# How many weight halves are split ahead in the second block of a fused two-block transformer

## The chip, the cores and the metric

The kernel runs on one core of one Trainium2 chip. The metric is device time in microseconds (us); smaller is better. Three runs of the kernel before took 713.87, 714.85 and 716.04 us, a median of 714.85 us.

## The reference

One sequence of 256 tokens, 1024 wide, in float32, goes through two blocks. Block 1 is an RMS norm, a stick-breaking attention beside a gated short convolution, and a mixture of 32 experts. Block 2 is the one that the change touches:

```
h = x @ w_in_2                          # 1024 -> 2560, split into q, k, v, u, z of 512 each
qh, kh = rope(q), rope(k)
attn = causal softmax(qh kh^T / 8) v    # 8 heads of 64
u, z = gelu(u), gelu(z)
sg = u * (tril(w_s) layer_norm(z) + b)  # per group of 64, in chunks of 128 tokens
merged = [rms_norm(attn), rms_norm(sg)]
x = layer_norm(alpha * x + merged @ w_out_2)
ffn = (silu(x @ w_gate) * (x @ w_up)) @ w_down      # hidden width 2816 = 22 chunks of 128
x = layer_norm(alpha * x + ffn)
```

## The kernel before

**Weights.** Every weight reaches the chip as a tile of 128 x 2048 float32, 1 MB. `Feed` (line 53) holds the tiles' order and a ring of buffers. Whenever a buffer is given back (`done`), the next tile's transfer is put on the SP queue. In block 2 the ring has six buffers.

**Splits.** Block 2 multiplies in float32r, with each operand as a high and a low part. `Split` (line 91) makes the parts of a weight half (128 x 1024) with two instructions of `hi_lo` (line 257): ScalarE copies the half into `whi` (L258), and VectorE subtracts that copy from the half into `wlo` (L259). The parts lie in nine buffers in block 2 (`WBUF2`), so half k+9 can be written only when TensorE has done with half k. `get(name)` hands out the next half. Before that it calls `ahead(n_got + n - less)`, which writes into the program the splits of all halves up to n ahead of the one handed out, with n = 9: the whole pool. `proj_tok` (L292) takes four halves for a projection of 512 columns, 12 matmuls of 512 columns each (L271). Behind the matmuls of half u it calls `ahead` once more and then the steps that the caller gave for that place (`then[u]`).

**Order of block 2.** The projections come as z, q, k, u, v (L1099 to L1115), 20 halves, numbered 0 to 19 here. Into them are woven, as `then` steps, the work on finished projections. Of these the prediction uses the path of z: `z_mean`, `z_sq` and `z_rstd` find each group's mean and deviation (the power of -1/2 runs on GpSimd, `rsqrt`, L249); `z_scale` (L981) multiplies on VectorE (L984), then multiplies and adds the layer norm's gain and bias on GpSimd (L985, L986); `z_mix(0)` (L988), the step behind the third half of k, multiplies the result by the spatial weights on TensorE (L992). `rope` (L941) turns q and k on VectorE, and adds on GpSimd (L951). Then follow the output projection (`wo2`, halves 20 to 27), the first layer norm (L1173 to L1247), and the feed-forward part, whose halves begin at 28. The first four of these are used inside the layer norm's section (`first_hidden`, L1212). At its end, L1247 splits up to nine ahead of half 32, so halves 33 to 40, since 32 is there by then. Then `gated(0)` and `gated(1)` (L1253) reduce the four results of `first_hidden`, which frees their PSUM banks, and `hidden(2)`, `hidden(3)` (L1264) do the next two hidden chunks. `hidden(3)` uses the two `pc` banks that `gated(1)` frees.

**Who sets the order.** Inside `tc.manual_schedule(...)` the named engines keep their instructions in the order of the program: around the whole z projection (L1089 to L1099) and around the layer norm (L1173 to L1247). Elsewhere a planner orders each engine's instructions: it plays the program through with times of its own, and gives an engine that has come free the instruction that stands earliest in the program among those that it takes to be ready. Each engine then runs its instructions strictly in the order so found.

Of the kernel before, what the change touches and what calls it, by code (L numbers as in the profile page):

```python
# [33 lines left out]
WBUF = 3  # L34
WBUF2 = 9
# [17 lines left out]
class Feed:  # L53


    def __init__(self, nc, order):
        self.nc = nc
        self.order = order
        self.free = []
        self.loaded = []  # L60
        self.n_loaded = 0
        self.slot = {}
# [18 lines left out]
    def get(self, name):  # L81
        _, t, s = self.loaded.pop([n for n, _, _ in self.loaded].index(name))
        self.slot[id(t)] = s
        return t
# [6 lines left out]
class Split:  # L91


    def __init__(self, feed, pool, units, hi_lo, n):
        self.feed, self.pool, self.units, self.hi_lo, self.n = feed, pool, units, hi_lo, n
        self.held = {}
        self.ready = []
        self.n_got = 0
# [11 lines left out]
            self.ready.append((name, hi, lo))  # L110

    def get(self, name, less=0):
        self.ahead(self.n_got + self.n - less)
        got, hi, lo = self.ready[self.n_got]
        assert got == name, (got, name)
        self.n_got += 1
        return hi, lo
# [3 lines left out]
def fused_blocks(ctx: ExitStack, tc: tile.TileContext, a, out):  # L121
# [10 lines left out]
    def pool(name, bufs=1, side=None, **kw):  # L132
        es = ExitStack()
        p = es.enter_context(tc.tile_pool(name=name, bufs=bufs, side=side, reuse_waits="tile", **kw))
        return es, p


    units_a, units_b, order = [], [], []
# [74 lines left out]
    feed = Feed(nc, order)  # L213
# [29 lines left out]
    def small(p, w, tag, bufs=2):  # L243
        ctr[0] += 1
        return p.tile([P, w], F32, tag=tag, name=f"{tag}_{ctr[0]}", bufs=bufs)
# [19 lines left out]
    def dense_tok(acc, ks, cols, xh, xl, t, first, last):  # L265

        tok = slice(t * P, (t + 1) * P)
        for i, (kc, hi, lo, o) in enumerate(ks):
            for n, (x_, w_) in enumerate(((xh, hi), (xh, lo), (xl, hi))):
                for c in cols:  # L270
                    mm(acc[c], x_[:, kc, tok], w_[:, o + c * 512:o + (c + 1) * 512],  # L271
                       start=first and i == 0 and n == 0, stop=last and i == len(ks) - 1 and n == 2)
# [18 lines left out]

    def proj_tok(W, name, xh, xl, then={}, new=bank):  # L292
        accs = [[new()] for _ in range(NT)]
        for u in range(4):
            hi, lo = W.get(name)
            for t in range(NT):
                dense_tok(accs[t], [(2 * u, hi, lo, 0), (2 * u + 1, hi, lo, 512)], (0,), xh, xl, t, u == 0, u == 3)
            if u in then:
                W.ahead(W.n_got + W.n)
                then[u]()  # L300
        return [c[0] for c in accs]

    def rows_proj(W, name, acc, xh, xl, k0, first, last, then={}):

        if not last:
            for u in range(2):
                hi, lo = W.get(name)
                for t in range(NT):
                    dense_tok(acc[t], [(k0 + u, hi, lo, 0)], (0, 1), xh, xl, t, first and u == 0, False)
                if u in then:  # L310
                    W.ahead(W.n_got + W.n)
                    then[u]()
            return
        ks = [(k0 + u,) + W.get(name, 2 * u) + (0,) for u in range(2)]
        for t in range(NT):
            for c in range(2):
                dense_tok(acc[t], ks, (c,), xh, xl, t, first, True)
                if 2 * t + c in then:
                    then[2 * t + c]()
# [34 lines left out]
    wes, wp = pool("w_a", bufs=WBUF, side="left")  # L354
# [20 lines left out]
    W = Split(feed, wp, units_a, two_halves, WBUF)  # L375
# [541 lines left out]
    wes, wp = pool("w_b", bufs=WBUF2, side="left")  # L917
    xes, xp = pool("x_b", side="left")
    ees, ep = pool("blk2", side="right")
    W = Split(feed, wp, units_b, hi_lo, WBUF2)  # L920
    x_hl = xp.tile([P, 2, KD, S], F32R, name="x2")
    xh, xl = x_hl[:, 0], x_hl[:, 1]
    mh = xp.tile([P, KD, S], F32R, name="mh2")
# [38 lines left out]
    def gelu(n, dst):  # L962
        for t in range(NT):
            act(dst[:, t, :], b2[n][t], AF.Gelu)
# [120 lines left out]
    def then(*steps):  # L1085

        return {i: (lambda fs=fs: [f(*a) for f, *a in fs]) for i, fs in enumerate(steps)}

    with tc.manual_schedule(engines=in_order):  # L1089
# [7 lines left out]
        for k in range(0, KD, 2):  # L1097
# [12 lines left out]
    v_sb = ep.tile([P, NT, 512], F32, tag="x2T1", name="v2")  # L1110
    gelu("u2", u_sb)
    nc.scalar.preload_act_table_set("natural_log_exp_and_others")
    b2["v2"] = proj_tok(W, "v2", xh, xl, then([(z_gate, 0), (soft_b, 0)], [(soft_a, 1), (z_gate, 1), (soft_c, 0)],
                                              [(soft_b, 1), (z_t, 0)], [(soft_d, 0), (soft_a, 2), (soft_c, 1)]))
    v_in()  # L1115
# [16 lines left out]
    def attn_rows(t, us, cols):  # L1132
        for u in us:
            dense_tok(acc[t], ks[u:u + 1], cols, mh, ml, t, u == 0, u == 3)
# [12 lines left out]
    def stats(t, c, combine):  # L1147
        if c == 0:
            ln[t] = fp.tile([P, 2, 6], F32, tag="bst", name="bst", bufs=2)
        o = xres[:, t, c * 512:(c + 1) * 512]  # L1150
        combine(t, c, o)
        nc.vector.bn_stats(out=ln[t][:, c, :], in_=o)  # L1152
        if c:
            mv = small(fp, 2, "mv")
            nc.vector.bn_aggr(out=mv, in_=ln[t])
            ve = small(fp, 1, "ve")
            ts(ve, mv[:, 1:2], 1e-5, None, op0=ALU.add)
            ln[t] = mv[:, 0:1], rsqrt(fp, ve)
# [14 lines left out]
    with tc.manual_schedule(engines=in_order):  # L1173
        for c in range(2):
            attn_rows(0, (3,), (c,))
            stats(0, c, add_mix)
        shift = small(fp, 1, "mr")
        stt(out=shift, in0=ln[0][0], scalar=-1.0, in1=ln[0][1], op0=ALU.mult, op1=ALU.mult)
        attn_rows(1, (0, 1), (0, 1))
        for cols in half:  # L1180
            act(xn[:, 0, cols], xres[:, 0, cols], AF.Identity, scale=ln[0][1], bias=shift)
        attn_rows(1, (2, 3), (0,))
        stats(1, 0, add_mix)

        def turned(src, t, k, z):

            for i in range(2):
                tr(z[:, k % 4 + i, :], src[:, t, (k + i) * P:(k + i + 1) * P], ident)

        def in_chunks(z):  # L1190
            return z.rearrange("p (k s) -> p k s", k=4)

        z0 = [in_chunks(bank_c()) for _ in range(2)]
        for j in range(4):
            turned(xn, 0, 2 * j, z0[j // 2])
        attn_rows(1, (2, 3), (1,))
        ws = [[W.get("fgu", 4 + 2 * f + i) for i in range(2)] for f in range(2)]
        zs = [[two_parts(new()) for _ in range(2)] for new in (bank, bank_c)]

        def split3(t, j, src):  # L1200
            ks = slice(2 * j, 2 * j + 2)
            hi_lo(xh[:, ks, tok[t]], xl[:, ks, tok[t]], src)

        def part0(j):

            x3 = fp.tile([P, 2, P], F32, tag="x3", name="x3", bufs=2)
            for i in range(2):
                kc = 2 * j + i
                act(x3[:, i, :], z0[j // 2][:, kc % 4, :], AF.Identity, scale=V("ln1_g", kc), bias=V("ln1_b", kc))
            split3(0, j, x3)  # L1210

        def first_hidden(t, j):  # L1212

            for kc in (2 * j, 2 * j + 1):
                f = slice(kc * P, (kc + 1) * P)
                for w, z in zip(ws, zs):
                    for (hi, lo), z_ in zip(w, z):
                        mm(z_[:, :, tok[t]], hi[:, f], both(x_hl, kc, tok[t]), start=kc == 0 and t == 0, stop=False,  # L1218
                           skip_group_check=True)
                        if t:  # L1220
                            mm(z_[:, 0, :], lo[:, f], xh[:, kc, :], start=False, stop=kc == KD - 1,
                               skip_group_check=True)

        ln1 = feed.get("ln1")
        g1, b1 = ln1[:, 0:D], ln1[:, D:2 * D]
        part0(0)
        stats(1, 1, lambda t, c, o: (add_mix(t, c, o), part0(1)))
        part0(2)
        centred(1, half[0], g1)
        part0(3)  # L1230
        for j in range(4):
            first_hidden(0, j)
        z1 = [in_chunks(bank_c()) for _ in range(2)]

        def part1(j):
            scaled(xres[:, 1, quarter[j]], 1, quarter[j], b1)
            turned(xres, 1, 2 * j, z1[j // 2])

        part1(0)
        for j in range(4):  # L1240
            if j < 3:
                part1(j + 1)
            split3(1, j, z1[j // 2][:, 2 * (j % 2):2 * (j % 2) + 2, :])
            if j == 0:
                centred(1, half[1], g1)
            first_hidden(1, j)
        W.ahead(W.n_got + W.n)  # L1247


    acc = None  # L1250
# [146 lines left out]
```

## Time and profile before

| what | value |
|---|---|
| median of three runs | 714.85 us (713.87 to 716.04) |
| the profiled execution | 713.62 us |
| its span, from the first to the last instruction | 711.9 us |
| TensorE busy | 661.3 us, 93% |
| VectorE busy | 368.2 us, 52% |
| ScalarE busy | 271.1 us, 38% |
| mean granted TensorE clock | 0.978 |

Times in the rows are microseconds from the start of the span. PE is TensorE's matmuls, DVE is VectorE, ACT is ScalarE, POOL is GpSimd. A row of a timeline shows the start, the duration, the engine, the line, the operation with what it writes and reads, and in brackets how long the engine had been idle before it and what ended the wait. "x16" means that 16 instructions are merged into the row. Matmuls are pipelined, so a row's duration can reach into the next. Block 2 begins with the matmul at 403.53 us and takes the rest of the span.

### The profile page before, as it was taken

The page shows a single profiled execution, that of the slowest core. Times are in us where ns is not written, and L with a number is a line of the kernel's source. Part 1 is how long each engine was busy: PE and PEld are TensorE (multiplying, and loading weights), DVE is VectorE, ACT ScalarE, POOL GpSimd, SP SyncE. Part 2 cuts the span into 40 slices and gives each one's busy share as a digit, 9 for nine tenths or more (in the row PEclk, how much of TensorE's full clock was granted, in tenths as well). Part 3 has the DMA queues.
Part 4 walks back from the last instruction along what each step waited for, and adds up shares of the span by engine and source line. Part 5 has one row for each costly group of instructions (what it writes and reads, how often), then busy time and mean ns, then how long its engine had stood idle before and what let it go on. Part 6 is the DMA issues. An engine that isn't in the chain of part 4 may idle for free. (4 is left out here: it accounts for less than half of the span.)

```text
span 711.9 us, 10413 instructions
## 1 busy us (share of the span) xinstructions
PE 661.3 (93%) x4249; PEld 516.7 (73%) x4249; DVE 368.2 (52%) x578; ACT 271.1 (38%) x413; POOL 43.9 (6%) x60
## 2 busy tenths in 40 slices
PE   8999999999999888998799598999979999999995
PEld 6888999999964444434256386877778888888884
DVE  6657555555521211212000488577578767667646
ACT  6567554444310000000000583477364444444410
POOL 2321100000000000000000006001100000000001
PEclk9999999999999999999899799999999999999998
DMA  8983479738879999999999784542146655555001
GB/s 341 410 338 119 147 303 347 258 122 344 365 298 394 421 420 419 419 420 417 418 418 416 269 319 155 193 162 66 54 180 234 231 189 192 200 193 178 1 0 60
DMA packets 27558, 185.63 MB, mean 261 GB/s; under 512 B 3312, under 2 KB 3824, under 8 KB 5872
## 3 DMA queue, kind: packets, MB, share of 16 engines
q1 hardware_dynamic: 27504, 184.89, 67.2%
q8 instruction: 36, 0.59, 0.3%
q14 instruction: 18, 0.15, 0.1%
HBM read 183.83 MB, written 1.05 MB: 260 GB/s over the span
## 5 line engine op out<-in xcount | busy, mean ns | idle before, releaser
L259 DVE TENSOR_TENSOR wlo<-w,whi 128x1024 fp32r<-128x1024 f32 (+1 forms) x151 | 185.4, 1237 | 84.3 <-ACT whi L258 83.1
L258 ACT ACTIVATE whi<-w 128x1024 fp32r<-128x1024 f32 (+1 forms) x151 | 157.3, 1057 | 165.9 <-PE pa_t L271 67.9
L286 PE MATMUL pc_t<-x,whi 128*128 128x512 f32 x320 | 114.9, 402 | 3.8 <-DVE fs L1255 3.8
L287 PE MATMUL pc_t<-x,wlo 128*128 128x256 f32 x320 | 90.4, 282 | 0.0
L286 PEld LDWEIGHTS pc_t<-x,whi 128*128 128x128 f32 x320 | 60.8, 190 | 19.0 <-ACT fs L1256 4.1
L806 PE MATMUL pc_t<-w,xg 128*32 128x512 f32 x512 | 62.0, 617 | 4.0 <-DMA w<-in_w_gu_dram 4.0
L287 PEld LDWEIGHTS pc_t<-x,wlo 128*128 128x128 f32 x320 | 61.1, 191 | 0.4
L836 ACT ACTIVATE h<-pc_t 128x256 f32<-128x256 f32 x8 | 3.1, 384 | 135.2 <-PE pc_t L755 110.5
L756 DVE TENSOR_TENSOR xg<-pc_t,vec 128x512 f32<-128x512 f32 (+2 forms) x18 | 11.4, 633 | 80.2 <-PE pc_t L755 80.2
L806 PEld LDWEIGHTS pc_t<-w,xg 128*32 128x32 f32 x512 | 14.5, 111 | 39.6 <-issue 26.0
L271 PE MATMUL pa_t<-whi,x 128*128 128x512 f32 x128 | 42.8, 403 | 0.0
L847 PEld LDWEIGHTS pa_t<-st,y 128*128 128x128 f32 x128 | 23.0, 189 | 21.9 <-DVE y L863 12.5
L847 PE MATMUL pa_t<-st,y 128*128 128x256 f32 x128 | 31.9, 392 | 6.3 <-DVE y L863 6.2
L280 PE MATMUL pc_t<-xh,wlo 128*128 128x256 f32 x128 | 36.2, 283 | 0.0
L279 PE MATMUL pc_t<-xl,whi 128*128 128x256 f32 x128 | 36.2, 283 | 0.0
L278 PE MATMUL pc_t<-xh,whi 128*128 128x256 f32 x128 | 36.2, 283 | 0.0
L806 PE MATMUL pc_t<-w,hT 128*32 128x512 f32 (+1 forms) x272 | 31.2, 574 | 4.1 <-ACT hT L842 4.1
L755 PEld LDWEIGHTS pc_t<-pr,xres 128*128 128x128 f32 x256 | 29.3, 192 | 7.8 <-PE pc_t L806 4.2
L755 PE MATMUL pc_t<-pr,xres 128*128 128x128 f32 x256 | 31.1, 278 | 0.9 <-DVE pr L746 0.9
L863 DVE COPY y<-pc_t 128x512 f32<-128x512 f32 x7 | 4.8, 692 | 50.8 <-PE pc_t L806 50.8
L271 PE MATMUL pa_t<-whi,fh 128*128 128x512 f32 x88 | 28.7, 392 | 0.0
L271 PE MATMUL pa_t<-wlo,fh 128*128 128x512 f32 x88 | 28.6, 391 | 0.0
(313 smaller groups left out, 1225.6 us busy)
## 6 DMA issues: line engine op xcount, KB each, us to landing
w<-in_w_gu_dram SPq DMA_DIRECT2D x64, 1024.0 KB, 19.4
w<-in_w_dn_dram SPq DMA_DIRECT2D x32, 1024.0 KB, 19.6
w<-in_w_in_dram SPq DMA_DIRECT2D x28, 1024.0 KB, 12.6
w<-in_w_ffn_dram SPq DMA_DIRECT2D x22, 1024.0 KB, 4.9
w<-in_w_fdn_dram SPq DMA_DIRECT2D x11, 1024.0 KB, 4.8
w<-in_w_out_dram SPq DMA_DIRECT2D x8, 1024.0 KB, 5.0
w<-in_w_in_dram SPq DMA_DIRECT2D x4, 512.0 KB, 12.2
w<-in_w_cv_dram SPq DMA_DIRECT2D x2, 1024.0 KB, 9.4
```

The lines of the kernel that those rows point to most:

```text
L258: act(hi, src, AF.Copy)
L259: tt(out=lo, in0=src, in1=hi.bitcast(F32), op=ALU.subtract)
L271: mm(acc[c], x_[:, kc, tok], w_[:, o + c * 512:o + (c + 1) * 512], start=first and i == 0 and n == 0, stop=last and i == len(ks) - 1 and n ...
L278: mm(acc, hi[:, f], xh[:, kc, :], start=kc == 0, stop=False)
L279: mm(acc, hi[:, f], xl[:, kc, :], start=False, stop=False)
L280: mm(acc, lo[:, f], xh[:, kc, :], start=False, stop=kc == nk - 1)
L286: mm(z, hi[:, f], x[:, :, kc, :], start=kc == 0, stop=False, skip_group_check=True)
L287: mm(z[:, 0, :], lo[:, f], x[:, 0, kc, :], start=False, stop=kc == nk - 1, skip_group_check=True)
L755: mm(zv[:, k, :], xres[:, t, kc * P:(kc + 1) * P], pr[:, t, :], start=t == 0, stop=t == 1)
L756: tt(out=xg[:, ks, :], in0=zv, in1=V("ffn_g")[:, ks].unsqueeze(2).to_broadcast([P, n, P]), op=ALU.mult)
L806: mm(out[sl, 0:n], x[:, sl], w[:, e * 512 + i * n:e * 512 + (i + 1) * n], start=start, stop=stop, skip_group_check=True)
L847: mm(acc[2 * c + k // 2][:, k % 2, :], ys[c][:, k * P:(k + 1) * P], st, start=False, stop=False, skip_group_check=True)
```

## The change

`Split` gets a distance `lead` of its own and a step `grow`. In block 2 `lead` begins at 5 (`WBUF + 2`) in place of 9, while the pool keeps its nine buffers. Ahead of the v projection `grow` is set to 1, so that each further `get` raises `lead` by one until it is 9. Each `get` in v then writes two splits into the program. At the end of the layer norm, L1247 no longer splits eight halves: it sets `lead` to 2, and from there every `get` raises it by one again. Block 1's `Split` has no `lead` given and works as before.

```diff
-    def __init__(self, feed, pool, units, hi_lo, n):
+    def __init__(self, feed, pool, units, hi_lo, n, lead=None):
         self.feed, self.pool, self.units, self.hi_lo, self.n = feed, pool, units, hi_lo, n
+        self.lead = lead or n
+        self.grow = 0
...
     def get(self, name, less=0):
-        self.ahead(self.n_got + self.n - less)
+        self.lead = min(self.n, self.lead + self.grow)
+        self.ahead(max(self.n_got + 1, self.n_got + self.lead - less))
...
             if u in then:
-                W.ahead(W.n_got + W.n)
+                W.ahead(W.n_got + W.lead)
                 then[u]()
...
-    W = Split(feed, wp, units_b, hi_lo, WBUF2)
+    W = Split(feed, wp, units_b, hi_lo, WBUF2, WBUF + 2)
...
     nc.scalar.preload_act_table_set("natural_log_exp_and_others")
+    W.grow = 1
     b2["v2"] = proj_tok(W, "v2", xh, xl, then([(z_gate, 0), (soft_b, 0)], [(soft_a, 1), (z_gate, 1), (soft_c, 0)],
...
             first_hidden(1, j)
-        W.ahead(W.n_got + W.n)
+        W.lead = 2
```

## Rows read from the trace of the kernel before

**Rows 1.** The page's first part, TensorE to GpSimd: busy us, share of the span, instructions.
```profile
PE 661.3 (93%) x4249; PEld 516.7 (73%) x4249; DVE 368.2 (52%) x578; ACT 271.1 (38%) x413; POOL 43.9 (6%) x60
```
**Rows 2.** TensorE's waits from 400 to 712: us in total, times, longest.
```profile
PE pc_t L286 <- DVE fs L1255: 3.8, 1, 3.8
PE pc_t L992 <- POOL z L986: 3.2, 1, 3.2
```
**Rows 3.** Windows: length, busy us of PE, PEld, DVE, ACT, POOL; granted clock; DMA.
```profile
440.00:450.00 10.00, 9.16 (x45) 8.03 (x46) 5.42 (x7) 2.03 (x3) 3.33 (x3) 0.83 0.32 104
...
530.00:540.00 10.00, 6.23 (x28) 5.17 (x28) 10.00 (x16) 6.28 (x10) 0.00 (x0) 0.83 0.88 327
```
**Rows 4.** The chain that ended last, around the first gap: start, us, what.
```profile
421.27 10.91 PE pa_t L271 x48
...
436.93 1.66 POOL z L985
438.66 2.13 POOL z L986
440.84 2.64 PE pc_t L992 x16
443.49 3.78 PE pa_t L271 x12
...
453.60 1.73 PE pc_t L992 x16
```
**Rows 5.** GpSimd's timeline from 390 to 445.
```profile
393.80 1.10 POOL L959 TENSOR_SCALAR_AFFINE_SELECT w<-w 128x1024 f32<-128x1024 f32 x1 [205.28 <-DMA w<-in_w_sp_dram]
429.31 4.01 POOL L249 TENSOR_TENSOR rs<-ms,mhalf 128x8 f32<-128x8 f32 x2 [34.41 <-DMA w<-in_w_out_dram]
...
442.83 1.27 POOL L986 TENSOR_TENSOR z<-z,w 128x512 f32<-128x512 f32 x1
```
**Rows 6.** VectorE's timeline from 430 to 440.
```profile
430.59 1.23 DVE L259 TENSOR_TENSOR wlo<-w,whi 128x1024 fp32r<-128x1024 f32 x1
...
433.31 2.35 DVE L259 TENSOR_TENSOR wlo<-w,whi 128x1024 fp32r<-128x1024 f32 x1 [0.23 <-ACT whi L258]
...
436.18 0.68 DVE L984 TENSOR_TENSOR z<-z,rs 128x512 f32<-128x512 f32 x1
...
437.38 2.29 DVE L259 TENSOR_TENSOR wlo<-w,whi 128x1024 fp32r<-128x1024 f32 x1
```
**Rows 7.** ScalarE's timeline, a split in the k projection.
```profile
437.65 1.06 ACT L258 ACTIVATE whi<-w 128x1024 fp32r<-128x1024 f32 x1 [1.66 <-PE pa_t L271]
```
**Rows 8.** TensorE's timeline from 520 to 538.
```profile
520.92 0.48 PE L286 MATMUL pc_t<-x,whi 128*128 128x512 f32 x1
...
529.93 0.40 PE L286 MATMUL pc_t<-x,whi 128*128 128x512 f32 x1
...
530.28 0.40 PE L286 MATMUL pc_t<-x,whi 128*128 128x512 f32 x1
...
534.56 0.77 PE L286 MATMUL pc_t<-x,whi 128*128 128x512 f32 x1 [3.77 <-DVE fs L1255]
...
537.64 0.28 PE L287 MATMUL pc_t<-x,wlo 128*128 128x256 f32 x1
```
**Rows 9.** ScalarE's timeline behind the layer norm.
```profile
522.36 9.58 ACT L258 ACTIVATE whi<-w 128x1024 fp32r<-128x1024 f32 x10
```
**Rows 10.** VectorE's timeline, layer norm and behind it.
```profile
507.42 0.75 DVE L1161 SCALAR_TENSOR_TENSOR xres<-pa_t,rs,xres 128x512 f32<-128x512 f32 x1 [0.57 <-PE pa_t L271]
...
521.62 0.42 DVE L259 TENSOR_TENSOR x<-pc_t,x 128x256 fp32r<-128x256 f32 x1 [3.13 <-ACT x L258]
...
523.44 9.18 DVE L259 TENSOR_TENSOR wlo<-w,whi 128x1024 fp32r<-128x1024 f32 x8 [0.52 <-ACT whi L258]
532.53 0.68 DVE L1255 TENSOR_REDUCE fs<-pa_t 128x256 f32<-128x512 f32 x1
```
**Rows 11.** The window of the v projection, columns as in Rows 3.
```profile
462.00:478.00 16.00, 16.00 (x91) 12.16 (x87) 11.74 (x29) 13.07 (x32) 1.24 (x2) 1.00 0.46 164
```

More of the change, by code (lines that the diff above doesn't have):

```diff
@@ L310, in rows_proj @@
                 if u in then:
-                    W.ahead(W.n_got + W.n)
+                    W.ahead(W.n_got + W.lead)
                     then[u]()
@@ L1246, in fused_blocks @@
             first_hidden(1, j)
-        W.ahead(W.n_got + W.n)
+        W.lead = 2
     acc = None
```

## The prediction

> **What bounds the kernel now.** The page's first part comes first: TensorE is busy 93% of the span and VectorE 52% [rows 1], so a change on VectorE and ScalarE pays only where TensorE waits for them. Next I read TensorE's waits in block 2. Two of them touch code that the change moves: 3.8 us on VectorE's reduce of the first gated chunks (L1255), and 3.2 us on GpSimd's last step on z (L986) [rows 2]. The chain of waits and the timelines then show what stands in front of each.
>
> At the first gap `z_mix(0)` starts at 440.84, as soon as L986 is over [rows 4]. L986 and L985 follow `z_scale(0)`, which VectorE runs only at 436.18, behind two `wlo` splits, at 430.59 and 433.31. A third split runs beside GpSimd's two steps [rows 6]. GpSimd had both powers done at 433.32 (429.31 + 4.01) [rows 5], the first, which is the one needed, by about half of that pair, 431.3.
>
> At the second gap VectorE runs eight `wlo` in a row from 523.44, and the first reduce of `gated(0)` only behind them, at 532.53 [rows 10]; ScalarE runs ten `whi` [rows 9]. TensorE needs the banks of `gated(1)` for its next chunk and stands still for 3.77 us [rows 8].
>
> Behind each gap TensorE is also granted less clock: 0.83 in the mean of each of the two windows [rows 3], so a part of each stretch is at 1.2 and the rest at 2.4 GHz.
>
> **The change part by part.** No split is removed: in both kernels 1.06 us of ScalarE [rows 7] and about 1.23 us of VectorE [rows 6] per half. What changes is where each split stands in the program. The planner need not leave it there. It moves work far forward when it takes its input to be there: GpSimd's mask of the spatial weights (L959, written behind the z projection) runs at 393.80, ahead of block 2 [rows 5], and matmuls of `hidden(2)` run at 520.92, inside the layer norm [rows 8]. All nine buffers stay, so a split can still float forward to where its buffer comes free. What it loses is its rank: a split that stands later no longer beats a step that is ready at the same time.
>
> *The v-projection end of it, and the transfers.* Four splits fewer stand in z, and four more in v (two with each `get`). At the place in v this is 4 x 1.06 = 4.2 us of ScalarE and 4 x 1.23 = 4.9 us of VectorE. In the 16 us of v these have 2.93 and 4.26 us free [rows 11]. If all four stayed there, ScalarE would be over by 1.3 and VectorE by 0.7 us; 1.3 us is the upper end. I take 0, since the window before has VectorE idle for 4.58 of 10 us and ScalarE for 7.97 [rows 3], and the splits can float into it; the halves ready in stock (five at least) are a second cover. A tile's transfer follows its second half's split, so transfers start up to two tiles later; the DMA share is 0.46 in v and 0.32 before it [rows 11, 3], so I take 0 there too. The lower end is 0 for both: no wait of TensorE in v is there to be removed.
>
> *The first gap.* A half of a projection takes 12 matmuls of 10.91 / 48 = 0.227 us, 2.73 us [rows 4], and with each half one split falls due in either kernel, so VectorE's load between 429 and 438 need not fall. But in program order the splits written by then now stand behind `z_scale(0)`: with `lead` 9 those at 430.59 and 433.31 were ahead of it. Without these two, `z_scale(0)` comes 1.23 + 2.35 = 3.58 us earlier, at 432.6, and the power was ready at 431.3. That covers the gap of 3.23 us. Further, ScalarE's in-order queue stands behind a `whi` that waits 1.66 us for TensorE to give a buffer back [rows 7]; the squares of z were queued behind such waits, and they come earlier too. The least is a gain of 0, if the splits keep their places by floating. The most is the whole gap: 3.23 us, and the slow clock behind it. For that, `z_mix` took 2.64 instead of 1.73 us (0.91), and the next 12 matmuls 3.78 instead of 2.73 (1.05) [rows 4]. Together 3.23 + 1.96 = 5.2 us. I take all of it, since the work removed from the front is longer than the gap. What is late next is the second half of z: its last step ends at 442.83 + 1.27 = 444.1 [rows 5] and its `z_mix` runs at 453.60 [rows 4], so it has over 9 us to spare, some 4 of them after TensorE has moved forward by 5.2.
>
> GpSimd's add took 2.13 us beside the third split [rows 4] and 1.27 us with VectorE out of the way [rows 5]; a `wlo` took 2.35 beside GpSimd and 1.23 without [rows 6]. The Trainium skill (page "SBUF — State Buffer", section "Who interferes with whom") says of this that a VectorE instruction with two SBUF inputs and a GpSimd instruction that reads SBUF share a port, and whichever starts first holds it while the other blocks; the two rows agree. The rule speaks against the change, as it leaves a floated `wlo` free to land ahead of either step of GpSimd: by it each would wait up to 1.23 us, so L985 and L986 would take up to 2 x (1.27 + 1.23) = 5.0 us instead of the 3.8 of today, and 1.2 us of the gap would come back. By the row alone they stay at 3.8 or fall to 2.5. I stay with the row; 1.2 us goes into the forecast's own range.
>
> *The second gap.* Eight splits no longer stand ahead of `gated(0)`. With `lead` at 2, half 32 is ready, and `get` for 32 writes 33 and 34 behind both gated chunks. TensorE works on a half in eight pairs of 530.28 - 529.93 = 0.35 us. Half 33's last began at 530.28; three pairs of half 32 ran early, from 520.92, and 12 pairs counted back from 530.28 give the end of `first_hidden`, 526.0 [rows 8]. Half 32 then gives it 5 x 0.35 = 1.8 us. Half 33 must be split by 527.8. Its buffer, last used in the output projection, is free, and ScalarE and VectorE have nothing of the gated chunks until 526.0, so 33 to 35 float into 522.4 to 526: 1.06 + 1.23 us for the first, and then one per 1.23. The four reduces of 0.68 us [rows 10] follow, and the banks are free by 526 + 4 x 0.68 + 1.23 = 530.0, in time for 530.65. So 3.77 us go, and with them the slow clock: the nine matmuls from 534.56 to 537.64 took 3.08 us, and at 0.35 a pair they take 1.63, a loss of 1.45 [rows 8]. Together 5.2 us. If no split floats, half 33 comes behind four reduces, two products and two low parts (0.42 each, as the one at 521.62), 4.4 us, and takes 1.23 itself: it is ready at 531.6, 3.8 us after 527.8, and the gap is as long as before. That is the lower end, a gain of 0. What is late next is the stock of halves, which is 2 or 3 instead of 9. A hidden chunk takes 2 x 2.84 us of TensorE and, on VectorE, two splits, two reduces and two small steps of about 0.42, 4.7 us. So VectorE gains on TensorE and the stock grows.
>
> *The layer norm.* Halves 33 to 36 (buffers of the output projection) are now free to float into it. One `wlo` in the 0.57 us gap at 507.42 would push the next step by 0.7; the 3.13 us in front of 521.62 hold two without loss [rows 10]. The least is 0, the most 4 x (1.06 + 1.23) = 9.2 us, if all eight pieces land on the chain one behind the other. I take 0.5, since the idle stretches hold most of them.
>
> *Sum.* -5.2 - 5.2 + 0.5 = -9.9 us on the profiled execution: 713.62 to 703.7, of which 1.7 lie outside the span in both kernels. The median of the runs was 1.23 above the profiled one, so I forecast 704.9 us, own range 703 to 707.5.
>
> **Rivals.**
> 1. *Splits float so well that the first gap stays.* The planner fills all nine buffers as early as before, `wlo` keeps its places, and only the second gap goes: 714.85 - 5.2 + 0.5 = 710.1 us. For it: the buffers, not the distance, hold `whi` back today [rows 7]. Against it: rank decides wherever both are ready.
> 2. *The layer norm takes what its end gives, the first gap goes.* Some four or five pieces on the chain: 714.85 - 5.2 = 709.7 us.
> 3. *It doesn't do what it says.* The planner puts splits back in front of both places, or half 33 comes late: 714.85, within 1 us.
> 4. *Slower.* Splits 33 to 36 land in the layer norm's chain, on ScalarE in front of the normalising and on VectorE in front of the halves of x. All eight pieces cost 9.2 us, and a TensorE idle that long loses clock, 1.45 as at the second gap; less the 5.2 gained, and with the first gap unchanged: 714.85 + 9.2 + 1.45 - 5.2 = 720.3 us. It turns to slower from five pieces on (5 x 1.14 = 5.7 against 5.2). For it: VectorE's gaps there are short and the planner fills any. Against it: long stretches are idle on both engines just behind.
>
> **Chances.** Forecast 0.48, rival 1 0.22, rival 2 0.06, rival 3 0.10, rival 4 0.14. Faster by over 0.3% (2.1 us, about what a measurement tells from no change): 0.48 + 0.22 + 0.06 = 0.76. Within it 0.10, slower 0.14. The range 702.5 to 715 leaves out rival 4 and half of rival 3.
>
> **What would show it.** Right: no wait for L986 over 1 us and `z_scale(0)` ahead of 434 on VectorE; the reduces of L1255 at about 526 with at most one or two `wlo` ahead; no wait of `hidden(3)`; granted clock 1.00 in both places. Wrong: a wait of TensorE on `wlo` or `whi` behind the layer norm, `wlo` between the steps of the layer norm with TensorE idle beside them, or waits on splits in v.

## The result, and the profile after

The changed kernel takes 708.76 us (median of 6 runs, 707.85 to 711.07) where the kernel before took 714.07 us (713.73 to 716.04) beside it: a ratio of 0.9923, 95% interval 0.9904 to 0.9943. The forecast was 704.9, with an own range of 703 to 707.5, so the time lies above that range: the gain is 5.3 us where 9.9 were expected. Lines of the program stand three to five further down than before: the low part of a split is L263, the first reduce of the gated chunks L1260, the last step on z L990.

First TensorE's waits from 395 us on, as in [rows 2]: both gaps are gone from the list, and two entries of the layer norm are new or longer (before, `xn` cost 0.4 us and `x` 1.3). The wait ahead of z is there in both kernels: 8.5 us before, 8.8 after.

```profile
PE pc_t L275 <- DVE wlo L263: 8.8, 1, 8.8
PE pa_t L1223 <- DVE x L263: 3.6, 3, 1.5
PE pc_t L1193 <- ACT xn L1186: 2.5, 1, 2.5
```

The first gap on VectorE, which answers to [rows 6] (start, us, instruction):

```profile
427.67 1.21 DVE L263 TENSOR_TENSOR wlo<-w,whi 128x1024 fp32r<-128x1024 f32 x1
...
431.46 1.04 DVE L988 TENSOR_TENSOR z<-z,rs 128x512 f32<-128x512 f32 x1
...
433.02 2.32 DVE L263 TENSOR_TENSOR wlo<-w,whi 128x1024 fp32r<-128x1024 f32 x1
435.27 1.78 DVE L988 TENSOR_TENSOR z<-z,rs 128x512 f32<-128x512 f32 x1
```

GpSimd behind it, as in [rows 5]:

```profile
426.17 2.50 POOL L253 TENSOR_TENSOR rs<-ms,mhalf 128x8 f32<-128x8 f32 x1 [32.12 <-DVE ms L258]
...
432.58 1.69 POOL L989 TENSOR_TENSOR z<-z,w 128x512 f32<-128x512 f32 x1 [0.63 <-DVE z L988]
434.34 2.17 POOL L990 TENSOR_TENSOR z<-z,w 128x512 f32<-128x512 f32 x1
```

And TensorE, as in [rows 4]; this row has no bracket, so nothing was waited for:

```profile
438.15 1.89 PE L996 MATMUL pc_t<-z,w 128*128 128x64 f32 x16
```

No split stands within 2.5 us ahead of `z_scale(0)` any more. GpSimd ends at 436.51, 1.64 us before TensorE comes for the result.

Now the layer norm on VectorE, to be read against [rows 10]. In the kernel before no `wlo` stood between any two of these steps. There `ve` followed `mv` directly:

```profile
505.57 0.21 DVE L1155 BATCH_NORM_AGGREGATE mv<-bst 128x2 f32<-128x12 f32 x1
505.82 0.15 DVE L1157 TENSOR_SCALAR ve<-mv 128x1 f32<-128x1 f32 x1
```

In the changed kernel:

```profile
501.19 0.21 DVE L1160 BATCH_NORM_AGGREGATE mv<-bst 128x2 f32<-128x12 f32 x1
501.41 1.23 DVE L263 TENSOR_TENSOR wlo<-w,whi 128x1024 fp32r<-128x1024 f32 x1
502.55 0.15 DVE L1162 TENSOR_SCALAR ve<-mv 128x1 f32<-128x1 f32 x1
502.77 1.23 DVE L263 TENSOR_TENSOR wlo<-w,whi 128x1024 fp32r<-128x1024 f32 x1
504.44 0.16 DVE L1183 SCALAR_TENSOR_TENSOR mr<-mv,rs 128x1 f32<-128x1 f32 x1 [0.44 <-POOL rs L253]
...
509.13 1.23 DVE L263 TENSOR_TENSOR wlo<-w,whi 128x1024 fp32r<-128x1024 f32 x1
510.27 0.42 DVE L263 TENSOR_TENSOR x<-x,x 128x256 fp32r<-128x256 f32 x1
...
511.21 1.21 DVE L263 TENSOR_TENSOR wlo<-w,whi 128x1024 fp32r<-128x1024 f32 x1
...
525.58 0.69 DVE L1260 TENSOR_REDUCE fs<-pa_t 128x256 f32<-128x512 f32 x1 [2.60 <-PE pa_t L1226]
```

ScalarE in the same stretch:

```profile
500.32 1.06 ACT L262 ACTIVATE whi<-w 128x1024 fp32r<-128x1024 f32 x1 [5.12 <-PE pa_t L275]
501.68 1.06 ACT L262 ACTIVATE whi<-w 128x1024 fp32r<-128x1024 f32 x1 [0.30 <-PE pa_t L275]
504.63 1.52 ACT L1186 ACTIVATE xn<-xres,mr,rs 128x512 f32<-128x512 f32 x2 [1.89 <-DVE mr L1183]
...
508.04 1.05 ACT L262 ACTIVATE whi<-w 128x1024 fp32r<-128x1024 f32 x1
508.99 0.41 ACT L262 ACTIVATE x<-x 128x256 fp32r<-128x256 f32 x1
...
509.98 1.06 ACT L262 ACTIVATE whi<-w 128x1024 fp32r<-128x1024 f32 x1
```

GpSimd there, the power for the norm's deviation, in the changed kernel and then in `held_behind_norm`, an experiment below in which no split floats into the norm:

```profile
502.83 1.57 POOL L253 TENSOR_TENSOR rs<-ve,mhalf 128x1 f32<-128x1 f32 x1 [4.17 <-DVE ve L1162]
```

```profile
499.54 0.55 POOL L253 TENSOR_TENSOR rs<-ve,mhalf 128x1 f32<-128x1 f32 x1 [3.04 <-DVE ve L1162]
```

TensorE there:

```profile
505.50 1.36 PE L1193 MATMUL pc_t<-ident,xn 128*128 128x128 f32 x8 [2.50 <-ACT xn L1186]
...
510.74 0.50 PE L1223 MATMUL pa_t<-x,whi 128*128 128x256 f32 x2 [1.53 <-DVE x L263]
...
513.11 0.51 PE L1223 MATMUL pa_t<-x,whi 128*128 128x256 f32 x2 [1.15 <-DVE x L263]
```

All four floated halves, 33 to 36, are here: four `whi`, and four `wlo` that stand between the norm's own steps on VectorE. At the other end, the reduce at 525.58 has no split ahead of it and waits for TensorE.

Windows (columns as in [rows 3]) of the two places of the gaps, and of the v projection against [rows 11]:

```profile
435.00:445.00 10.00, 10.00 (x58) 8.63 (x57) 10.00 (x8) 4.15 (x5) 5.79 (x3) 1.00 0.42 134
460.00:476.00 16.00, 16.00 (x86) 12.15 (x85) 11.97 (x31) 11.86 (x32) 0.56 (x1) 1.00 0.40 141
...
520.00:530.00 10.00, 10.00 (x72) 9.20 (x71) 5.05 (x9) 5.28 (x9) 0.00 (x0) 1.00 0.01 2
```

TensorE is busy throughout at the full clock, 1.00, where the two gap windows of before had 0.83.

**Block 2 by stages.** Five stretches between TensorE's rows in each profiled execution (us). A: first matmul of z to `z_mix(0)`. B: from there to the first matmul of the output projection. C: to the first turned `xn`. D: to the last matmul of `first_hidden`. E: to the first matmul of the down projection. What follows E took 170.2 to 170.3 us in all twelve.

| kernel | z begins at | A | B | C | D | E |
|---|---|---|---|---|---|---|
| before | 403.53 | 37.31 | 36.39 | 30.52 | 18.17 | 15.73 |
| after | 404.15 | 34.00 | 34.70 | 32.65 | 20.48 | 10.37 |
| z_part_only | 403.44 | 34.72 | 34.70 | 30.51 | 18.16 | 16.79 |
| norm_part_only | 404.88 | 36.76 | 37.98 | 32.65 | 22.69 | 10.37 |
| held_behind_norm | 402.44 | 33.54 | 34.70 | 30.51 | 18.18 | 10.37 |
| held_norm_only | 406.21 | 37.66 | 36.40 | 30.51 | 18.17 | 10.37 |
| lead_8 | 403.33 | 34.57 | 34.80 | 30.53 | 18.15 | 10.37 |
| lead_7 | 403.78 | 33.93 | 34.81 | 30.55 | 18.16 | 10.37 |
| two_float | 403.21 | 33.66 | 34.69 | 32.65 | 19.04 | 10.37 |
| placed | 404.98 | 34.60 | 34.69 | 30.51 | 18.17 | 10.37 |
| no_growth_in_v | 405.02 | 33.63 | 35.77 | 29.38 | 20.74 | 11.43 |
| held_again | 402.67 | 34.80 | 34.70 | 30.51 | 18.17 | 10.37 |

From before to after: A and B -5.0, C and D +4.4, E -5.4, the start of z +0.6; together -5.3, which is 711.9 to 706.6 in the span. A varies by 1.3 us between kernels whose code there is the same (33.54 and 34.80 in one kernel run twice, `held_behind_norm` and `held_again`). That goes with the granted clock at the start of z: over 402 to 410 us it is 0.76 in the first of these two and 0.57 in the second, and z begins there within 0.23 us. The start of z varies by up to 4 us, in code that the edits don't touch. B to E repeat within 0.1 where the code is the same, but for stretches with a lower clock. Behind the first gap B is 37.98 in `norm_part_only` (clock 0.72 over 440 to 452 us) against 36.39 before (0.86 over 439.2 to 451.2). Behind the second E is 16.79 in `z_part_only` (0.77 over 525.6 to 540.6) against 15.73 before (0.89 over 530 to 545).

### The profile page after: what moved, and what is told of

The parts are those of the page before. It is cut to its first block, busy times and chain, and to the rows that moved or that the text cites. A ratio compares the mean times of both kernels' runs of the same rounds, so it can differ in the third digit from the quotient of the medians.

```text
span 706.6 us, 10411 instructions
## 1 busy us (share of the span) xinstructions
PE 658.1 (93%) x4249; PEld 514.9 (73%) x4249; DVE 367.7 (52%) x578; ACT 270.5 (38%) x413; POOL 46.7 (7%) x60
## 3 DMA queue, kind: packets, MB, share of 16 engines
HBM read 183.83 MB, written 1.05 MB: 262 GB/s over the span
## 5 line engine op out<-in xcount | busy, mean ns | idle before, releaser
L263 DVE TENSOR_TENSOR wlo<-w,whi 128x1024 fp32r<-128x1024 f32 (+1 forms) x151 | 186.0, 1239 | 84.7 <-ACT whi L262 84.3
L759 PEld LDWEIGHTS pc_t<-pr,xres 128*128 128x128 f32 x256 | 31.1, 201 | 8.7 <-PE pc_t L810 4.2
L759 PE MATMUL pc_t<-pr,xres 128*128 128x128 f32 x256 | 32.9, 289 | 0.9 <-DVE pr L750 0.9
```

The costliest lines, as they stand in the source:

```text
L263: tt(out=lo, in0=src, in1=hi.bitcast(F32), op=ALU.subtract)
L759: mm(zv[:, k, :], xres[:, t, kc * P:(kc + 1) * P], pr[:, t, :], start=t == 0, stop=t == 1)
```

## The experiments

My theory from the two traces: each gap closed by the amount forecast, and the layer norm took 4.4 us because the halves 33 to 36, no longer written behind the norm, floated into it. Against it: the loss could come from the early part (a smaller stock on entering the output projection), or the two ends could depend on each other. Each edit below is against the changed kernel.

**Each end alone.** `z_part_only` keeps the lead of five and the growth in v and splits up to nine behind the norm, as before:

```diff
-        W.lead = 2
+        W.ahead(W.n_got + W.n)
```

> The changed kernel's distance of 5 from z to u, growing in v, but behind the layer norm the eight splits of the kernel before, ahead of the gated chunks. My theory (rank at the first gap pays 5.2 us; the second gap is a separate 5.2; the changed kernel's layer norm is late because splits 33 to 36 float into it): the first gap is gone, the layer norm is as short as before, the second gap of 3.8 us stands: 5.2 us less than before, about 708.9 against 714.1. Rival (the layer norm of the changed kernel is late because of the splits put off from z to v): the layer norm is some 4 us late here too, about 713.

Measured: 709.91 us, ratio 0.9921 [0.9904, 0.9938], 1.0 above my 708.9. The norm is unharmed (C 30.51, D 18.16) and the second gap stands whole, here in TensorE's timeline:

```profile
530.17 0.76 PE L290 MATMUL pc_t<-x,whi 128*128 128x512 f32 x1 [3.77 <-DVE fs L1260]
```

`norm_part_only` is the other end alone, with nine to begin with:

```diff
-    W = Split(feed, wp, units_b, hi_lo, WBUF2, WBUF + 2)
+    W = Split(feed, wp, units_b, hi_lo, WBUF2, WBUF2)
```

> The distance is 9 from z on, as before; only the end of the layer norm is changed (2, then one more with each half). My theory: the first gap stands, the second is gone (-5.2), and four floated splits make the layer norm some 4.2 us longer: about 713.1 against 714.1. Rival (the late layer norm comes from the part in z and v): no loss in the layer norm, about 708.9.

Measured: 715.41 us, ratio 0.9999 [0.9984, 1.0014]: no gain at all, 2.3 us worse than I expected. C is late by 2.13 us as in the changed kernel, so the early part has no share in that. D is 2.2 us longer still. TensorE's waits in the norm are not longer than in the changed kernel (the first row is the first gap, which stands):

```profile
PE pc_t L996 <- POOL z L990: 3.2, 1, 3.2
PE pa_t L1223 <- DVE x L263: 2.9, 3, 1.2
PE pc_t L1193 <- ACT xn L1186: 2.5, 1, 2.5
```

What is added in this profile is the clock. Windows of this kernel's norm, where TensorE stood still from 509.8 to 512.27:

```profile
510.00:512.00 2.00, 0.00 (x0) 0.00 (x0) 1.56 (x3) 0.60 (x1) 1.17 (x1) 1.00 0.76 217
512.00:514.00 2.00, 1.68 (x10) 1.40 (x11) 0.72 (x2) 1.93 (x5) 0.00 (x0) 0.93 0.73 307
514.00:516.00 2.00, 2.00 (x6) 1.52 (x6) 0.42 (x1) 2.00 (x5) 0.00 (x0) 0.50 0.00 0
```

After the 2.50 us wait the granted clock is 0.50, the 1.2 GHz level, and from 522 to 524, behind the wait of 1.15 us for `x`, it is 0.51. In the changed kernel the same wait of 2.50 us was followed by 1.00 throughout 500 to 520. So the floated splits cost 4.4 us, or 6.6 with the clock in this profile. The twelve executions of this kernel spread from 712.95 to 717.30 us, and the profile is of the one at 717.30. Besides D, it has B 1.6 us longer than the kernel before and z beginning 1.35 us later. Four of the twelve took 712.95 to 713.50, about the 713.1 that I expected; whether the clock fell in those, no trace shows.

**The four halves kept out of the norm.** `held_behind_norm` writes 33 to 36 inside the norm's section, behind its last matmuls. There the engines keep the program's order, so they can't float forward:

```diff
+        W.ahead(W.n_got + 5)
         W.lead = 2
```

> The changed kernel, but the splits of halves 33 to 36 are written at the end of the layer norm's ordered section, so that they cannot float into it; 37 and later follow as in the changed kernel. My theory: the layer norm is as short as in the kernel before (3.4 us from the first half's statistics to the first turned matmul, and 1.7 us of waits in all), both gaps are gone, four splits ahead of the gated chunks are not enough to bring the second back: 4 to 4.5 us less than the changed kernel, about 704.3. Rival (something else in the changed kernel makes the layer norm long): 708.5, as the changed kernel.

Measured: 702.09 us, ratio 0.9818 [0.9800, 0.9835]; a second measurement, on another chip, gave 702.77 and 0.9831 [0.9815, 0.9846]. C and D are back to 30.51 and 18.18, and A, B and E stay as in the changed kernel. TensorE's waits behind the start of z:

```profile
PE pa_t L1223 <- DVE x L263: 1.2, 2, 0.9
PE pc_t L1193 <- ACT xn L1186: 0.4, 1, 0.4
```

VectorE behind the norm: four splits ahead of the reduce, instead of eight in [rows 10] and none in the changed kernel, and no wait of TensorE for it.

```profile
516.89 4.63 DVE L263 TENSOR_TENSOR wlo<-w,whi 128x1024 fp32r<-128x1024 f32 x4 [0.52 <-ACT whi L262]
521.44 0.68 DVE L1261 TENSOR_REDUCE fs<-pa_t 128x256 f32<-128x512 f32 x1
```

My expectation of 704.3 was 2.2 too high; in this kernel's profile z began 1.7 us earlier than in that of the changed one, and A was 0.5 shorter. The float was the loss, and this version beats both kernels.

`held_norm_only` is the same with nine to begin with (both edits above), so the second gap alone, without the loss.

> Distance 9 from z on, as before; behind the layer norm four splits in the ordered section instead of eight, then 2 and one more with each half. My theory: only the second gap goes, with no loss in the layer norm: 5.2 us less than before, about 708.9. Rival (the second gap needs the gated chunks ahead of all splits): the gap keeps half of its length, about 711.5.

Measured: 708.93 us, ratio 0.9901 [0.9882, 0.9921]. With `z_part_only` the two ends add up: 0.79% and 0.99% against 1.82% for both.

**How many splits ahead make the first gap.** `lead_8` and `lead_7` have the hold of `held_behind_norm`, and begin with 8 and 7 instead of 5:

```diff
-    W = Split(feed, wp, units_b, hi_lo, WBUF2, WBUF + 2)
+    W = Split(feed, wp, units_b, hi_lo, WBUF2, 8)
...
+        W.ahead(W.n_got + 5)
         W.lead = 2
```

> As the kernel that holds 33 to 36 behind the layer norm, but with a distance of 8 instead of 5 from z to u. In the changed kernel z_scale(0) stood 27.3 us behind the first matmul of block 2 and GpSimd's last step on z ended at 32.4; before, 32.7 and 37.3; TensorE asks for it at about 34.0. Theory A (each split put off frees its 1.2 us wherever it stood): one split less gives 35.9, so a wait of about 2 us stays, with or without slow clock behind it: 2 to 4 us more than with 5, 705 to 706.5. Theory B (as predicted: only the two splits right in front of z_scale(0) count): one of the two stays, the gain is about half, a wait near 1.5 us. Theory C (it is the distance as such, 9 being the whole pool, that makes ScalarE wait for buffers): 8 is as good as 5, about 702.5.

> The same with a distance of 7. Theory A: two splits less give 34.6, a wait of about 0.6 us, no slow clock: about 703. Theory B: both splits in front of z_scale(0) are gone and so is the wait: about 702.5. Theory C: about 702.5 too. If the wait is still over 1.5 us, all three are wrong on the place where the splits cost.

Measured: `lead_8` 703.94 us, ratio 0.9849 [0.9826, 0.9873], and the wait is 0.80 us; `lead_7` 704.49 us, ratio 0.9859 [0.9836, 0.9883], and the wait is 0.19. VectorE of `lead_8`:

```profile
430.50 1.21 DVE L263 TENSOR_TENSOR wlo<-w,whi 128x1024 fp32r<-128x1024 f32 x1
...
432.90 0.98 DVE L988 TENSOR_TENSOR z<-z,rs 128x512 f32<-128x512 f32 x1
```

`z_scale(0)` runs 29.57 us behind the first matmul of z, against 32.65 before and 27.31 in the changed kernel. The first split fewer takes away the dearer of the two, the one that ran for 2.35 us beside GpSimd at 433.31 [rows 6], and with it 2.4 of the 3.2 us; the one at 430 stays. In `lead_7` that one stays too, at 430.29, and `z_scale(0)` runs 28.90 us behind the first matmul of z. So the wait shrinks with the distance, 3.23, 0.80, 0.19 and none at 9, 8, 7 and 5, and most of it was one split. None of the three theories had the wait of `lead_8` (about 2 us, near 1.5, none); B, by which one of the two splits in front stays, is the nearest, but it had both of them gone at 7. The times don't tell the steps apart: the intervals of 8 and 7 overlap for the most part, and `lead_7` missed the 702.5 to 703 expected.

**Two halves floating, two not.** In `two_float` the splits of 35 and 36 may not be issued before the first reduce and silu of `gated(0)`; 33 and 34 float:

```diff
-            self.hi_lo(hi, lo, w[:, h * 1024:(h + 1) * 1024])
+            (self.late if len(self.ready) in (35, 36) and self.late else self.hi_lo)(hi, lo, w[:, h * 1024:(h + 1) * 1024])
...
+    def behind(marks, *x):
+        with tc.issue_after(marks[0].ins), tc.issue_after(marks[1].ins):
+            hi_lo(*x)
...
+        marks = red(out=s, in_=zg.rearrange("p b s -> p s b"), axis=AX.X, op=ALU.add), act(s, s, AF.Silu)
+        W.late = W.late or (lambda *x: behind(marks, *x))
```

> The changed kernel, but the splits of halves 35 and 36 are tied behind the first reduce and silu of gated(0); 33 and 34 float into the layer norm as they did. My theory (33 and 34 cost 2.1 us ahead of the normalising, 35 and 36 another 2.3 us between the halves of x): the first turned matmul of xn is as late as in the changed kernel (32.7 us behind the first wo2 matmul), from there to the end of first_hidden it takes 18.2 us as before, not 20.5: 2.3 us less than the changed kernel, about 706.3, and about 2.1 more than with all four held. Rival (the delays overlap, and either pair costs nearly all): about 708.3.

Measured: 706.29 us, ratio 0.9885 [0.9861, 0.9908]. The time is the one expected, but D is not: C is late by the full 2.13 us with two floated halves, so 33 and 34 make the first loss; D is 19.04 instead of 18.2, all the waits for `x` but the one of 0.9 us are gone, and what is left above 18.17 is clock: the 2.50 us wait was followed by 0.50 here, too.

```profile
506.00:508.00 2.00, 2.00 (x7) 1.61 (x6) 0.55 (x2) 1.97 (x6) 0.00 (x0) 0.50 0.00 0
```

**Is there room in the norm at all?** `placed` writes 33 and 34 into the norm by hand, in front of the third of the four transposed pieces of its second half, where VectorE is idle for 3.13 us [rows 10], and 35 and 36 behind its last matmuls:

```diff
             if j < 3:
                 part1(j + 1)
+            if j == 2:
+                W.ahead(W.n_got + 3)
...
+        W.ahead(W.n_got + 5)
         W.lead = 2
```

> The changed kernel with 33 and 34 written by hand into the layer norm's section, where VectorE stood idle for 3.1 us (ahead of the third pair of x of the second half), and 35 and 36 at its end. My theory (the layer norm does have room for two splits, it is only the planner that puts them elsewhere): no loss in the layer norm, the same time as with all four at the end, 702 to 703. Rival (any split inside it costs): 1 to 2.5 us more.

Measured: 703.44 us, ratio 0.9837 [0.9816, 0.9859], no different from `held_behind_norm` by the intervals. C 30.51 and D 18.17: two splits within the norm cost nothing there.

```profile
515.44 2.35 DVE L263 TENSOR_TENSOR wlo<-w,whi 128x1024 fp32r<-128x1024 f32 x2
518.65 0.42 DVE L263 TENSOR_TENSOR x<-pc_t,x 128x256 fp32r<-128x256 f32 x1 [0.86 <-ACT x L262]
```

**The growth in v.** `no_growth_in_v` is `held_behind_norm` with the growth begun only behind the norm:

```diff
-    W.grow = 1
...
-        W.lead = 2
+        W.ahead(W.n_got + 5)
+        W.lead, W.grow = 2, 1
```

> As held_behind_norm (the layer norm's section splits halves 33 to 36 ahead behind its last matmuls, lead 2 from there), but lead stays at five through v and the output projection and only grows from the gated chunks on. My theory: the growth in v neither earns nor costs anything, since the buffers and not the distance hold the splits back there: 702 us as held_behind_norm (within 1 us of it on the same chip), z_mix(0) to the first matmul of the output projection 34.7 us, output projection 30.5 us, no wait of TensorE in either. Rival A: the growth pays, because it fills the stock that the output projection lives on (its halves are 12 matmuls of 0.227 us, 2.7 us, against 1.06 + 1.23 us of split beside the norms): without it TensorE waits for wlo there, at one or two halves by 1 to 2 us each, 704 to 706 us. Rival B: the four more splits in v are a load on VectorE (4.9 us) that delays the gates and the second z: without them v is up to 1.3 us shorter, 700.8 us.

> The same kernel as held_behind_norm, run again beside no_growth_in_v: 702.1 us if its first measurement holds, a ratio of 0.982 to the kernel before. If the spread of the part ahead of block 2 (z projection starting at 402.4 to 406.2 us in the profiles so far) made that first measurement good by chance, 703.5 to 704 us as lead_8 and placed gave.

Measured: `no_growth_in_v` 708.68 us, ratio 0.9903 [0.9882, 0.9924]; `held_again` beside it 702.77. Rival A had the direction, but none of my three theories had the place. B and C together are 65.15 us against 65.21, so v and the output projection neither gain nor lose. D is 2.6 and E 1.1 us longer. D, for this on VectorE:

```profile
505.44 3.50 DVE L263 TENSOR_TENSOR wlo<-w,whi 128x1024 fp32r<-128x1024 f32 x3 [0.54 <-ACT whi L262]
508.85 0.42 DVE L263 TENSOR_TENSOR x<-x,x 128x256 fp32r<-128x256 f32 x1
```

With lead still at five, halves 29 to 31 are first written by the four `get` calls at the head of the norm's section (L1202 takes 28 to 31), where the program's order holds, so the splits stand in front of the halves of `x`; TensorE waits for `x` 4.6 us in all, against 1.3 in `held_again`. E is longer for another reason: half 32 is now split only behind the norm. In `held_again` it is ready, and three pairs of its matmuls, 1.05 us at 0.35 a pair, run early, inside the norm (first row); in `no_growth_in_v` its first matmul comes behind the last of `first_hidden` (second row, another kernel).

```profile
515.85 0.48 PE L290 MATMUL pc_t<-x,whi 128*128 128x512 f32 x1
```

```profile
524.66 0.40 PE L290 MATMUL pc_t<-x,whi 128*128 128x512 f32 x1
```

The growth earns its place by having halves 29 to 32 split before the norm needs them. Of the 5.9 us between the medians the profiles show 2.4 in block 2 (D and E, less 1.2 in A); another 2.35 is the later start of z (405.02 against 402.67), in code that is the same, and is not explained.

## Why the prediction was right and where it was wrong

**What bounds the kernel**: right. Both gaps were what the change removes.

**The first gap**, -5.2: right. A and B gave 3.3 + 1.7 = 5.0, slow clock included. Counted from the first matmul of z, `z_scale(0)` moved by 5.3 us rather than 3.58, as the squares and powers came earlier too. The forecast counted on both splits; `lead_8` shows that the later one alone makes 2.4 of the 3.2 us. The port rule that was weighed (the Trainium skill, page "SBUF — State Buffer", section "Who interferes with whom") shows in the rows: a `wlo` floated to 433.02 and took 2.32 us beside GpSimd's two steps on the first half of z, and these took 1.69 + 2.17 = 3.86 us. That is the 3.8 of the row and not the 5.0 of the worst case that was worked out from the rule. The steps of the second half took 2.12 and 2.16, where the last took 1.27 before [rows 5]. It cost TensorE nothing, as GpSimd was 1.64 us early.

**The second gap**, -5.2: right, 5.36 in E. The forecast had the reduces at 526 with half 33 split in time; they ran at 525.58. But half 33 was not split in the idle stretch from 522.4 to 526 that the forecast gave it: it had floated into the norm, to 500.32, together with 34 to 36.

**The v projection's end**, 0: right for v itself. What I left out is what lead five would have done without it, in the norm; it didn't show in the forecast, since the change has the growth.

**The layer norm**, +0.5: wrong, it was 2.13 + 2.31 = 4.4 us. This is the term that failed: 704.9 with 4.4 in place of 0.5 is 708.8. That this is the measured time to 0.1 us is partly luck: so corrected, the gain is 6.0 us, and 5.3 were measured, with z beginning 0.6 us later in the profile. I took the idle stretches to hold most of the eight pieces. The room is there, as `placed` shows, but the planner didn't put the splits there. The `whi` at 500.32 and 501.68 start as matmuls of the output projection end, on which they wait, and that was in the tightest chain of the norm. That the planner goes by the time at which it takes a buffer to be free fits these rows; it was not tested by itself. The trace has the sign that the prediction gave for being wrong: `wlo` between the steps of the norm, with TensorE idle beside them. Piece by piece: the `wlo` at 501.41 stands between `mv` and `ve`, which start 1.36 us apart instead of 0.25, 1.11 more; the one at 502.77 runs beside GpSimd's power, which took 1.57 us where it takes 0.55 in `held_behind_norm`, 1.02 more. Together 2.13, as much as C. The Trainium skill's port rule, named above, agrees with this row: the power reads SBUF while a two-input `wlo` runs, and it ends 0.40 us behind that. I weighed the rule at z and not here, and here it cost 1 us. The pieces at 508.04 to 511.21 put the two waits for `x` up from 0.24 and 0.15 us (as in `held_again`) to 1.53 and 1.15, 2.3 more, against the 2.31 of D.

**The rivals.** Rival 4 named the mechanism of the loss, the right halves, engines and places. It had the price at twice what it was (9.2, each piece added to the chain; for one thing, the `whi` of 33 and 34 ran while ScalarE waited for `mr` anyway) and needed the first gap to stay. Had it stayed, there would have been no gain: that is `norm_part_only`, 715.41. Rival 1 has its time (710.1) near the result for another reason; the first gap did go. Rival 2's sum (709.7, the norm taking what its end gives) is nearer to what happened than the forecast is: 4.4 of 5.4 us were taken. I gave rivals 4 and 2 chances of 0.14 and 0.06, too little for a mechanism that [rows 5, 8] had shown at work.

## What to carry to other kernels

To write work later does not make it run later. Where a planner may pull it forward, it lands wherever its buffer comes free, and a critical chain of short steps on several engines is such a place. Work that is taken out of one queue needs a floor as well as a rank: hold it behind the last step of the tight section, or set it by hand into an idle stretch, and count what a shared port does to the small steps on the neighbouring engine. A distance that is made smaller must be large again before the next section in which the order is fixed.

## What was not expected of the hardware

The same wait of TensorE, 2.50 us for `xn`, was followed by a granted clock of 0.50 in `norm_part_only` and `two_float`, and by 1.00 in the changed kernel. What decides it is open; it is worth 0.9 us (D of `two_float`) to 2.2 us (D of `norm_part_only`).

TensorE also ran at a lower clock without any wait before it. From 190 to 210 us, 200 us ahead of block 2, the three profiles of kernels that begin with nine splits show 0.93, the other nine 1.00, with TensorE's instructions in the same order. The kernel before, and then the changed one:

```profile
190.00:210.00 20.00, 19.07 (x154) 12.91 (x154) 8.59 (x45) 1.21 (x4) 0.00 (x0) 0.93 0.70 270
```

```profile
190.00:210.00 20.00, 19.07 (x166) 12.87 (x165) 8.75 (x47) 2.08 (x4) 0.00 (x0) 1.00 0.80 317
```

It is no part of the gain that can be shown: z begins at 403.53, 404.88 and 406.21 us in the three and at 402.44 to 405.02 in the nine, and the experts before it run with the transfers at a share of 1.01 (300 to 350 us). Why the initial lead should reach so far back is open.
